# A third of the modulation products moved from VectorE to GpSimd and ScalarE, with weight slots from a free list

## The chip, the cores and the metric

The kernel runs on one core of a Trainium2 chip. The metric is the device time of one launch in microseconds (us); before the change it is 2290.78 us, the median of three runs from 2289.36 to 2290.9. Engines are named as in the profile: PE is TensorE (PEld its weight loads), DVE VectorE, ACT ScalarE, POOL GpSimd, SP the engine whose queue issues the transfers.

## What is computed

A decoder trunk of two layers over 256 tokens with 2048 features, all in float32. Each layer is a token mixer (a gated linear recurrence in layer 0, sparse attention in layer 1) followed by an MLP; so there are four sub-layers, s = 0 to 3. Every sub-layer is modulated by a shift, a scale and a gate that come from one conditioning vector:

```python
cond = jax.nn.silu(c)
mod = jnp.einsum('bd,jde->bje', cond, ada_w[layer]) + ada_b[layer]
shift, scale, gate = jnp.split(mod, 3, axis=-1)
h = x * (1.0 + scale[:, 0, None]) + shift[:, 0, None]
y = mixer(h)
x = _layer_norm(DN_ALPHA * x + (1.0 + gate[:, 0, None]) * y, ln_w, ln_b)
h = x * (1.0 + scale[:, 1, None]) + shift[:, 1, None]
y = sq_relu_mlp(h, mlp_w1, mlp_w2)
x = _layer_norm(DN_ALPHA * x + (1.0 + gate[:, 1, None]) * y, ln_w, ln_b)
```

The modulation needs, per sub-layer, 3 x 2048 dot products of length 2048 with `cond`: a matrix of weights is read once for a single vector.

## The kernel before

**The stream.** Some 620 MB of weights pass through the kernel once. They come as a list of items, most of them a unit of 128 partitions x 2048 numbers (1 MB), in an order written out in `build`: `merge` lays one list evenly into another. `Builder.prefetch` issues a unit's transfer on SP's queue (L104) into one of six slots of the tile `raw`, in turn, while fewer than six are in hand. `Builder.pump` takes the units in the order of the stream:

- A unit of modulation weights (kind "a", input `in_ada`, 192 of them: 48 for each sub-layer, in three parts of 16) holds 128 outputs, one on a partition. One DVE instruction (L120) multiplies it with `cond`, which lies on every partition, and its accumulator sums the products into one column of the tile `mod`.
- A unit of a matrix product (kind "w") is split into two float32r parts, half a unit at a time: ACT rounds it into `whi` (L135), DVE subtracts to get `wlo` (L136). They go into a ring of 16 pieces of 512 columns, from which PE takes them: three matmuls (L193 to L195) for each product.

**The order of instructions** is set when the program is built, by a clock of the builder's own: `step` moves it on by a fixed time for each piece that PE takes (1.31 us), a unit counts as arrived 3.0 us after the one before, and generators (`spawn`) are resumed when their time has come. On the chip each engine then runs its queue strictly in that order and waits on semaphores.

**Where modulation is waited for.** When the last unit of a batch is through, a hook runs: `make_ss` makes the columns `hA` and `hB` on DVE (L427 to L436), with which ACT modulates the activations (L454), which are then split (ACT L496, DVE L497) and multiplied. Sub-layer 0 takes its 32 shift and scale units in five groups (`GROUPS0`: 4, 4, 4, 2 and 2 feature tiles, so 8, 8, 8, 4 and 4 units, each followed by the weights of four products for these features). Sub-layer 1 takes them in four groups of 8 (`GROUPS1`), the first one laid into the recurrence before it. All other units (the gates, sub-layers 2 and 3) are laid into the stream of larger products, long before they are needed.

Between the groups of sub-layer 0 and those of sub-layer 1 stands the recurrence (convolution L801, gates L850, scan L873 and the operations between them, on DVE and ACT), with 24 units laid in.

Of the kernel before, what the change touches and what calls it, by code (L numbers as in the profile page):

```python
# [12 lines left out]
AF = mybir.ActivationFunctionType  # L13
OP = mybir.AluOpType
# [16 lines left out]
RAW = 6  # L31
# [5 lines left out]
GROUPS1 = ((0, 4), (4, 8), (8, 12), (12, 16))  # L37
UNIT_US = 3.0


class Item:
    def __init__(self, kind, src, col=None, then=None, width=2048):
        self.kind, self.src, self.col, self.then, self.width = kind, src, col, then, width
        self.group = 0
        self.done = False
        self.run = None
        self.pieces = {"w": width // 512, "g": 2}.get(kind, 0)


class Builder:  # L50
    def __init__(self, ctx, tc, a, out):
        self.tc, self.nc, self.a, self.out = tc, tc.nc, a, out
        nc = self.nc
        self.const = ctx.enter_context(tc.tile_pool(name="const", bufs=1))
        self.pool = ctx.enter_context(tc.tile_pool(name="work", bufs=1))
        self.psum = ctx.enter_context(tc.tile_pool(name="psum", bufs=1, space=PSUM))
        self.dram = ctx.enter_context(tc.tile_pool(name="dram", bufs=1, space=DRAM))
        self.raw = self.const.tile([128, RAW, 2048], F32, name="raw")
        self.whi = self.const.tile([128, RING, 512], F32R, name="whi")
        self.wlo = self.const.tile([128, RING, 512], F32R, name="wlo")  # L60
        self.now = 0.0
        self.tasks = []
        self.items = []
        self.di = self.pi = 0
        self.cons = self.prod = 0
        self.slot = self.inflight = 0
        self.arrive = []
        self.uid = 0

# [1 line left out]
    def t4(self, shape, dtype=F32):  # L71
# [13 lines left out]

# [1 line left out]
    def set_stream(self, items):  # L87
# [7 lines left out]
    def prefetch(self):  # L95
        while self.di < len(self.items) and self.inflight < RAW:
            it = self.items[self.di]
            if it.kind == "d":
                it.run()
            else:  # L100
                it.raw = self.raw[:, self.slot % RAW, :]
                self.slot += 1
                self.inflight += 1
                self.nc.sync.dma_start(out=it.raw[:, :it.width], in_=it.src)  # L104
            last = self.arrive[-1] if self.arrive else 0.0
            self.arrive.append(max(last, self.now + 1.5) + UNIT_US * it.width / 2048)
            self.di += 1

    def pump(self):
        nc = self.nc  # L110
        while self.pi < len(self.items):
            it = self.items[self.pi]
# [5 lines left out]
            r = it.raw  # L118
            if it.kind == "a":
                nc.vector.scalar_tensor_tensor(r, r, self.one, self.cond, op0=OP.mult, op1=OP.mult, accum_out=it.col)  # L120
            elif it.kind == "raw":
# [19 lines left out]
            self.pi += 1  # L141
            self.inflight -= 1
            self.prefetch()
            if it.then:
                it.then()

# [1 line left out]
    def spawn(self, gen, delay=0.0):  # L148
# [28 lines left out]

# [1 line left out]
    def piece(self, i):  # L179
# [6 lines left out]
    def head(self, kind):  # L186
        """The unit that is next in the stream, as it came."""
        self.until(lambda: self.items[self.pi].kind == kind and not self.items[self.pi].done and self.arrive[self.pi] <= self.now)
        return self.items[self.pi], self.items[self.pi].raw
# [20 lines left out]
    def gemm_ws_outer(self, act, dones, kinds, groups):  # L210
        """Several chunks of columns side by side, a few tiles of the contraction at a time."""
        bs = [[self.bank([128, 2, 256], kind) for _ in range(2)] for kind in kinds]
# [13 lines left out]
    def gemm_as(self, act, done, stagger=None, kind="g"):  # L226
        b = [self.bank([128, 512], kind) for _ in range(2)]
        if not stagger:
# [10 lines left out]
            return  # L239
        # the first token tile runs ahead of the second by as many tiles of weights as the ring holds  # L240
        c0 = self.cons
# [16 lines left out]

# [1 line left out]
    def new_act(self):  # L260
# [17 lines left out]
def build(ctx, tc, a, out):  # L278
# [4 lines left out]

# [1 line left out]
    cond = const.tile([128, 2048], F32, name="cond")  # L285
# [22 lines left out]

    # silu(c), on every partition
    ones = const.tile([1, 128], F32, name="ones")  # L310
# [10 lines left out]

# [1 line left out]
    state = {}  # L323

    def ada_items(s, part, tiles=range(16), then=None):
        its = [Item("a", a["ada"][s, part * 16 + k], col=mods[s][:, part * 16 + k:part * 16 + k + 1]) for k in tiles]
        if then:
            its[-1].then = then
        return its

# [22 lines left out]
    def hook(key):  # L353
        return lambda: hooks[key]()
# [16 lines left out]
    for k0, k1 in GROUPS0:  # L371
        ks = range(k0, k1)
        stream += ada_items(0, 0, ks)
        if k0 % 4 == 0:
            stream.append(x_item(k0 // 4))
        stream += ada_items(0, 1, ks, hook(("h0", k0, k1)))
        stream += [w_part("lru_in", (i,), k0, k1) for i in (4, 0, 5, 1)]
# [4 lines left out]
    def ss_group(k0, k1):  # L382
        ks = range(k0, k1)
        return ada_items(1, 0, ks) + ada_items(1, 1, ks, hook(("h1", k0, k1)))

# [13 lines left out]
    m0 = mlp_items(0)  # L399
    stream += merge(m0[16:], ada_items(1, 2, then=hook(("gate", 1))) + ada_items(2, 0) + ada_items(2, 1, then=hook(("ss", 2))) + ada_items(2, 2, then=hook(("gate", 2))))  # L400
    nsa = []
# [11 lines left out]
    nsa += q_items + [W("nsa_out", n, g) for n in range(4) for g in range(4)]  # L413
    stream += merge(nsa, ada_items(3, 0) + ada_items(3, 1, then=hook(("ss", 3))))
    m1 = mlp_items(1)
    stream += m1[:16] + merge(m1[16:96], ada_items(3, 2, then=hook(("gate", 3)))) + m1[96:]

# [1 line left out]
    def ln_cols(s):  # L419
        return cols[:, C_LNW + 16 * s:C_LNW + 16 * s + 16], cols[:, C_LNB + 16 * s:C_LNB + 16 * s + 16]  # L420

    def make_ss(s, k0=0, k1=16):
        """h = zn * hA + hB, with zn the normalized rows before sub-layer s (its input where s is 0)."""
        m = mods[s]
# [19 lines left out]
    def modulate(s, k0, k1, rows, A):  # L444
        """Up to four feature tiles of the transposed rows become the two parts of the modulated ones."""
        make_ss(s, k0, k1)
# [46 lines left out]

# [1 line left out]
    def split(hi, lo, src):  # L495
        SC.activation(hi, src, AF.Copy)  # L496
        V.tensor_tensor(out=lo, in0=src, in1=hi.bitcast(F32), op=OP.subtract)  # L497

# [1 line left out]
    def residual_source(s):  # L500
# [4 lines left out]
    def ln_task(s, z, t, stats, A, fin=None, rows=None):  # L505
        """Normalizes the rows of token tile t and, with A, makes sub-layer s+1's modulated rows, transposed
        (or with rows, the transposed rows alone; or with fin, the last layer norm's w and b, the output)."""
        mv = B.small([128, 2], "mv")
# [79 lines left out]
    def residual_task(s, z):  # L588
        """The output of sub-layer s, zn w + b, goes to memory until the next layer norm."""
        for n in range(4):  # L590
# [11 lines left out]
    def proj(s, A_in, z, A_out, first=True, last=True, fin=None, rows=None, kinds="gggg"):  # L602
        """z += act @ W over four chunks of columns. The last part of a sub-layer applies the gate, adds the
        residual and normalizes."""
        act = B.act_as(A_in)
# [117 lines left out]

    # ================= layer 0: RG-LRU =================
    # softplus(-lambda) from a range-reduced exponential and the series of log1p
    sp2 = const.tile([128, 16], F32, name="sp2")
# [168 lines left out]

    # ================= MLP of layer 0 =================
    B.until(lambda: znT[3] is not None and znT[3][1] == 3)
# [4 lines left out]

    # ================= layer 1: sparse attention =================
    # relative bias by distance: row h, column 127 + distance
    oh = B.t4([33, 512])
# [4 lines left out]

    # compressed keys and values
    kc = const.tile([128, 4, 15], F32, name="kc")
# [4 lines left out]
    def compress(i):  # L917
        """Sixteen of the 32 positions in a block; the other sixteen come with the next unit."""
        j, h = divmod(i, 2)
# [89 lines left out]

    # branch gates  # L1010
    gbank = B.bank([128, 256], "g")
# [26 lines left out]

    # attention
    O = [None] * NK  # L1040
# [8 lines left out]
    def back(t, start, step, n, copies=None):  # L1049
        """The last axis of t walked backwards from start."""  # L1050
        dims = [list(d) for d in t.ap]
        mid = [0, copies] if copies else dims[1]
        return bass.AP(tensor=t.tensor, offset=t.offset + start, ap=[dims[0], mid, [-step, n]])
# [114 lines left out]

    # ================= MLP of layer 1 =================
    z_in = z  # L1170
# [69 lines left out]
```

## Time and profile before

| | before |
|---|---|
| median of the runs shown | 2290.78 us |
| profiled execution, first to last instruction | 2292.0 us |
| PE busy | 2198.1 us (96%) |
| DVE busy | 1672.3 us (73%) |
| ACT busy | 1057.2 us (46%) |
| POOL busy | 0.2 us |
| moved by the transfers | 623.95 MB, mean 272 GB/s |
| modulation units on DVE | 192, 447.7 us in all |

The profile gives no time for the profiled execution but the span of its instructions, 1.2 us above the median of the runs. The shares are means over stages that differ: a share says which engine is full only where it is read stage by stage. PE's busy time counts matmuls that stand in its pipeline waiting for operands, so the number of matmuls in a stretch says more than the busy time.

### The profile page before, as it was taken

To read this page: it belongs to the slowest core of one execution; us is meant where nothing else is said; L and a number is where in the kernel's file an instruction comes from. 1 tells how busy PE (TensorE), PEld (TensorE's weight loads), DVE (VectorE), ACT (ScalarE), POOL (GpSimd) and SP (SyncE) were. 2 spreads that over 40 slices of the span, in tenths; PEclk is the share of its full clock that TensorE was granted. 3 is DMA by queue.
4 is the path that set the end of the run, shared out by engine and by line. 5 is a ranking of instruction groups with operands and counts; after the bars stand their busy time and mean duration, and the time that the engine had idled before them with its cause. 6 is when DMAs were issued, how large, how long until landed. Compare 5 with 4: busy or idle time off the path is not lost.

```text
span 2292.0 us, 33881 instructions
## 1 busy us (share of the span) xinstructions
PE 2198.1 (96%) x13970; PEld 1966.2 (86%) x13970; DVE 1672.3 (73%) x1987; ACT 1057.2 (46%) x1383; POOL 0.2 (0%) x4
## 2 busy tenths in 40 slices
PE   4799998989999999999999999999999999999997
PEld 3798977978998998998789988788989989988986
DVE  8899999886777767778887688668766444454456
ACT  2356644364453453444443355536544534443541
POOL 0000000000000000000000000000000000000000
PEclk9899999999999999999999999999999999999999
DMA  9987888988878878788689775356788555555561
GB/s 371 411 331 286 338 328 322 373 346 341 306 302 321 298 273 310 294 302 319 234 292 349 293 272 214 132 192 219 281 308 307 190 190 189 191 184 185 208 250 37
DMA packets 98218, 623.95 MB, mean 272 GB/s; under 512 B 10909, under 2 KB 13405, under 8 KB 26896
## 3 DMA queue, kind: packets, MB, share of 16 engines
q1 hardware_dynamic: 98064, 621.80, 72.5%
q8 instruction: 109, 1.79, 0.3%
q14 instruction: 45, 0.37, 0.0%
HBM read 613.30 MB, written 8.45 MB: 271 GB/s over the span
## 4 chain that ended last, share of the span: by engine, by line
PE 84%; DVE 11%; ACT 2%; issue 2%; DMA 1%; DVEq 0%; SPq 0%; ACTq 0%
PE g L195 26%; PE g L194 26%; PE g L193 26%; DVE raw L120 5%; DVE wlo L136 2%; PE m L1124 1%; PE m L1090 1%; ACT whi L135 1%; DMA raw<-in_lru_in 1%; DVE s L801 1%; PE m L929 1%; PE m L1116 0%; PE m L1127 0%; DVE s L497 0%; ACT s L454 0%
## 5 line engine op out<-in xcount | busy, mean ns | idle before, releaser
L136 DVE TENSOR_TENSOR wlo<-raw,whi 128x1024 fp32r<-128x1024 f32 x721 | 872.1, 1222 | 512.4 <-ACT whi L135 510.9
L135 ACT ACTIVATE whi<-raw 128x1024 fp32r<-128x1024 f32 x721 | 754.7, 1057 | 911.7 <-PE g L195 454.2
L193 PE MATMUL g<-s,whi 128*128 128x256 f32 (+1 forms) x2768 | 781.1, 283 | 51.6 <-ACT s L496 50.0
L194 PE MATMUL g<-s,whi 128*128 128x256 f32 (+1 forms) x2768 | 780.4, 282 | 5.1 <-DVE s L497 5.1
L195 PE MATMUL g<-s,wlo 128*128 128x256 f32 (+1 forms) x2768 | 780.6, 283 | 3.2 <-DVE wlo L136 3.2
L193 PEld LDWEIGHTS g<-s,whi 128*128 128x128 f32 (+1 forms) x2768 | 523.1, 189 | 59.1 <-ACT s L496 53.0
L193 PE MATMUL g<-whi,s 128*128 128x512 f32 x1376 | 547.4, 398 | 5.4 <-ACT s L496 5.4
L194 PE MATMUL g<-wlo,s 128*128 128x512 f32 x1376 | 544.9, 396 | 0.0
L195 PE MATMUL g<-whi,s 128*128 128x512 f32 x1376 | 544.6, 396 | 0.3 <-DVE s L497 0.3
L194 PEld LDWEIGHTS g<-s,whi 128*128 128x128 f32 (+1 forms) x2768 | 525.8, 190 | 8.9 <-DVE s L497 6.8
L195 PEld LDWEIGHTS g<-s,wlo 128*128 128x128 f32 (+1 forms) x2768 | 525.1, 190 | 4.8 <-DVE wlo L136 3.8
L120 DVE SCALAR_TENSOR_TENSOR raw<-raw,one,cond 128x2048 f32<-128x2048 f32 x192 | 447.7, 2345 | 19.1 <-DMA raw<-in_ada 18.9
L193 PEld LDWEIGHTS g<-whi,s 128*128 128x128 f32 x1376 | 258.9, 188 | 70.2 <-ACT s L496 7.4
L195 PEld LDWEIGHTS g<-whi,s 128*128 128x128 f32 x1376 | 258.7, 188 | 64.8 <-DVE s L497 2.2
L194 PEld LDWEIGHTS g<-wlo,s 128*128 128x128 f32 x1376 | 258.9, 188 | 62.0 <-issue 0.8
L454 ACT ACTIVATE s<-s,hB,hA 128x256 f32<-128x256 f32 x32 | 16.7, 590 | 120.9 <-DVE hA L430 80.4
L194 PE MATMUL m<-s,whi 128*128 128x256 f32 x256 | 71.1, 278 | 0.0
L195 PE MATMUL m<-s,wlo 128*128 128x256 f32 x256 | 71.1, 278 | 0.0
L193 PE MATMUL m<-s,whi 128*128 128x256 f32 x256 | 70.8, 279 | 0.2 <-ACT whi L135 0.2
L497 DVE TENSOR_TENSOR s<-t,s 128x512 fp32r<-128x512 f32 x78 | 52.8, 685 | 1.5 <-ACT s L496 1.3
L675 ACT ACTIVATE t<-g 128x512 f32<-128x512 f32 x58 | 33.9, 588 | 34.7 <-PE g L195 34.7
L193 PEld LDWEIGHTS m<-s,whi 128*128 128x128 f32 x256 | 47.8, 188 | 0.5 <-ACT whi L135 0.4
(189 smaller groups left out, 1048.6 us busy)
## 6 DMA issues: line engine op xcount, KB each, us to landing
raw<-in_mlp_w SPq DMA_DIRECT2D x256, 1024.0 KB, 5.0
raw<-in_ada SPq DMA_DIRECT2D x192, 1024.0 KB, 6.6
raw<-in_lru_in SPq DMA_DIRECT2D x28, 1024.0 KB, 8.4
raw<-in_nsa_kv SPq DMA_DIRECT2D x24, 1024.0 KB, 5.3
raw<-in_lru_out SPq DMA_DIRECT2D x16, 1024.0 KB, 6.3
raw<-in_nsa_q SPq DMA_DIRECT2D x16, 1024.0 KB, 6.5
raw<-in_nsa_out SPq DMA_DIRECT2D x16, 1024.0 KB, 4.9
t<-in_lnrow SPq DMA_DIRECT2D x24, 256.0 KB, 6.2
```

The lines of the kernel that those rows point to most:

```text
L120: nc.vector.scalar_tensor_tensor(r, r, self.one, self.cond, op0=OP.mult, op1=OP.mult, accum_out=it.col)
L135: nc.scalar.activation(hi, src, AF.Copy)
L136: nc.vector.tensor_tensor(out=lo, in0=src, in1=hi.bitcast(F32), op=OP.subtract)
L193: mm(out, lhi, rhi, start=start, stop=False, skip_group_check=True)
L194: mm(out, lhi, rlo, start=False, stop=False, skip_group_check=True)
L195: mm(out, llo, rhi, start=False, stop=stop, skip_group_check=True)
L497: V.tensor_tensor(out=lo, in0=src, in1=hi.bitcast(F32), op=OP.subtract)
L675: SC.activation(r2, banks[b], AF.Relu)
L801: V.scalar_tensor_tensor(o[:, sh:], p[:, :256 - sh], tap(i, j), o[:, sh:], op0=OP.mult, op1=OP.add)
L929: T.matmul(hv, r[:, 128 * l:128 * l + 128], x[:, :, h:15 + h, l], start=(h == 0 and l == 0), stop=(h == 1 and l == 15))
L1090: T.matmul(ps, qT[:, h, 128 * t:128 * t + 128], kT[g // 2][:, g % 2, :, 0:K], start=True, stop=True)
L1124: T.matmul(po, vt[br][:, kt, 128 * g:128 * g + 128], pT[:, br, kt], start=first, stop=False)
```

## The change

Every third unit of modulation weights (counted over the whole program by `turn`) is taken by a generator, `ada_pool`, unless the one before is still on its way: GpSimd multiplies the unit with `cond` in place, and after 5.5 us on the builder's clock (`POOL_US`) ACT copies the products onto themselves with its accumulator, which sums them into the column of `mod`. Meanwhile `pump` goes on with the next units. Since units are no longer finished in the order of the stream, a slot is handed back by number to a free list, and a hook runs when all units of its batch are through, not behind the last one. In the built program 64 of the 192 units go this way. Lines of the changed kernel: transfers L108, DVE's modulation product L130, `whi` and `wlo` L145 and L146, GpSimd's product L164, ACT's sum L166, `hA` and `hB` L456 to L460, modulation L483, split L525 and L526.

```diff
+POOL_EVERY = 3
+POOL_US = 5.5
...
-        self.slot = self.inflight = 0
+        self.free = list(range(RAW))
+        self.turn = 0
         self.arrive = []
         self.uid = 0
+        self.pooled = False
...
-        while self.di < len(self.items) and self.inflight < RAW:
+        while self.di < len(self.items) and self.free:
             it = self.items[self.di]
             if it.kind == "d":
                 it.run()
             else:
-                it.raw = self.raw[:, self.slot % RAW, :]
-                self.slot += 1
-                self.inflight += 1
+                it.slot = self.free.pop(0)
+                it.raw = self.raw[:, it.slot, :]
                 self.nc.sync.dma_start(out=it.raw[:, :it.width], in_=it.src)
...
             if it.kind == "a":
+                self.turn += 1
+                if self.turn % POOL_EVERY == 0 and not self.pooled:
+                    self.pooled = True
+                    self.pi += 1
+                    self.spawn(self.ada_pool(it))
+                    continue
                 nc.vector.scalar_tensor_tensor(r, r, self.one, self.cond, op0=OP.mult, op1=OP.mult, accum_out=it.col)
...
             self.pi += 1
-            self.inflight -= 1
-            self.prefetch()
-            if it.then:
-                it.then()
+            self.release(it)
+
+    def release(self, it):
+        self.free.append(it.slot)
+        self.prefetch()
+        if it.batch:
+            it.batch[0] -= 1
+            if not it.batch[0] and it.batch[1]:
+                it.batch[1]()
+
+    def ada_pool(self, it):
+
+        self.nc.gpsimd.tensor_tensor(out=it.raw, in0=it.raw, in1=self.cond, op=OP.mult)
+        yield POOL_US
+        self.nc.scalar.activation(it.raw, it.raw, AF.Copy, accum_out=it.col)
+        self.pooled = False
+        self.release(it)
...
-        stream += ada_items(0, 0, ks)
+        shift, scale = ada_items(0, 0, ks), ada_items(0, 1, ks)
+        batch_of(shift + scale, hook(("h0", k0, k1)))
+        stream += shift
         if k0 % 4 == 0:
             stream.append(x_item(k0 // 4))
-        stream += ada_items(0, 1, ks, hook(("h0", k0, k1)))
+        stream += scale
...
-        return ada_items(1, 0, ks) + ada_items(1, 1, ks, hook(("h1", k0, k1)))
+        return batch_of(ada_items(1, 0, ks) + ada_items(1, 1, ks), hook(("h1", k0, k1)))
```

The units of sub-layers 2 and 3 are gathered into batches in the same way. The order of the stream itself stays.

Two places show how the queues change. The first is ACT's queue between the first and the second group of sub-layer 0 (`s_...` are activations, `whi` the rounded weights). Before:

```order
L135 ACTIVATE whi<-raw 128x1024
L454 ACTIVATE s_301<-s_301,hB_95,hA_91 128x256 [waits DMAHW0_49,DVE_49]
L454 ACTIVATE s_301<-s_301,hB_95,hA_91 128x256 x3
L135 ACTIVATE whi<-raw 128x1024 [waits DMAHW5_49,PE_49,Activation_49]
L496 ACTIVATE s_465<-s_301 128x1024 [waits Activation_49]
```

and in the changed kernel:

```order
L145 ACTIVATE whi<-raw 128x1024
L166 ACTIVATE raw,mod_87<-raw 128x2048 [waits Pool_49] x3
L483 ACTIVATE s_303<-s_303,hB_95,hA_91 128x256 [waits DMAHW0_49,DVE_49]
L483 ACTIVATE s_303<-s_303,hB_95,hA_91 128x256 x3
L145 ACTIVATE whi<-raw 128x1024 [waits DMAHW5_49,PE_49]
L525 ACTIVATE s_470<-s_303 128x1024 [waits Activation_49]
```

Three sums of GpSimd's products now stand ahead of the group's modulation, each waiting for GpSimd; everything behind them waits too. The second place is DVE's queue in the same group, up to the first `wlo`. Before:

```order
L120 SCALAR_TENSOR_TENSOR raw,mod_87<-raw,one,cond 128x2048 [waits DMAHW6_49,DVE_49]
L120 SCALAR_TENSOR_TENSOR raw,mod_87<-raw,one,cond 128x2048 [waits DMAHW7_49,DVE_49]
L427 TENSOR_TENSOR mod_87<-mod_87,cols 128x4 [waits DVE_49]
L431 COPY hB_95<-mod_87 128x4 [waits DVE_49]
L120 SCALAR_TENSOR_TENSOR raw,mod_87<-raw,one,cond 128x2048 [waits DMAHW1_49]
L120 SCALAR_TENSOR_TENSOR raw,mod_87<-raw,one,cond 128x2048 [waits DMAHW2_49]
L120 SCALAR_TENSOR_TENSOR raw,mod_87<-raw,one,cond 128x2048 [waits DMAHW3_49]
L120 SCALAR_TENSOR_TENSOR raw,mod_87<-raw,one,cond 128x2048 [waits DMAHW4_49]
L427 TENSOR_TENSOR mod_87<-mod_87,cols 128x4 [waits DVE_49]
L430 TENSOR_SCALAR hA_91<-mod_87 128x4 [waits DVE_49]
L136 TENSOR_TENSOR wlo<-raw,whi 128x1024 [waits DMAHW5_49,PE_49,Activation_49]
```

and in the changed kernel:

```order
L130 SCALAR_TENSOR_TENSOR raw,mod_87<-raw,one,cond 128x2048 [waits DMAHW5_49]
L130 SCALAR_TENSOR_TENSOR raw,mod_87<-raw,one,cond 128x2048 [waits DMAHW6_49,DVE_49]
L456 TENSOR_TENSOR mod_87<-mod_87,cols 128x4 [waits DVE_49,Activation_49]
L460 COPY hB_95<-mod_87 128x4 [waits DVE_49]
L130 SCALAR_TENSOR_TENSOR raw,mod_87<-raw,one,cond 128x2048 [waits DMAHW1_49]
L130 SCALAR_TENSOR_TENSOR raw,mod_87<-raw,one,cond 128x2048 [waits DMAHW2_49]
L130 SCALAR_TENSOR_TENSOR raw,mod_87<-raw,one,cond 128x2048 [waits DMAHW4_49]
L456 TENSOR_TENSOR mod_87<-mod_87,cols 128x4 [waits DVE_49,Activation_49]
L459 TENSOR_SCALAR hA_91<-mod_87 128x4 [waits DVE_49]
L146 TENSOR_TENSOR wlo<-raw,whi 128x1024 [waits DMAHW5_49,PE_49,Activation_49]
```

Of the group's eight products five stay on DVE, and the small additions on `mod` (L456), which waited for DVE alone, now wait for ACT's sums as well.

## Rows read from the trace of the kernel before

**Rows 1.** The page: span, and part 1, each engine's busy time.
```profile
span 2292.0 us, 33881 instructions
PE 2198.1 (96%) x13970; PEld 1966.2 (86%) x13970; DVE 1672.3 (73%) x1987; ACT 1057.2 (46%) x1383; POOL 0.2 (0%) x4
```

**Rows 2.** Busy time of each engine by stage; stretch, its length, then engines with counts.
```profile
core 0: us, PE busy (x) PEld busy (x) DVE busy (x) ACT busy (x) POOL busy (x), PEclk, DMA share, GB/s
0.00:34.90 34.90, 7.19 (x8) 2.49 (x8) 29.52 (x67) 3.28 (x3) 0.20 (x4) 1.00 0.92 367
...
67.30:99.70 32.40, 24.81 (x192) 24.31 (x192) 29.16 (x30) 10.60 (x13) 0.00 (x0) 0.89 1.00 404
...
139.00:300.00 161.00, 153.98 (x1090) 144.61 (x1089) 157.54 (x188) 116.70 (x167) 0.00 (x0) 0.99 0.82 314
...
398.90:431.20 32.30, 32.30 (x276) 32.30 (x276) 29.29 (x34) 8.74 (x11) 0.00 (x0) 1.00 0.91 357
431.20:463.60 32.40, 28.30 (x223) 27.68 (x221) 29.18 (x30) 10.61 (x13) 0.00 (x0) 0.95 0.99 386
...
500.00:1110.00 610.00, 610.00 (x3758) 544.13 (x3757) 447.62 (x426) 274.97 (x306) 0.00 (x0) 1.00 0.81 309
```

**Rows 3.** Timeline of DVE, third group of sub-layer 0: start, duration, instruction.
```profile
67.32 0.17 DVE L430 TENSOR_SCALAR hA<-mod 128x4 f32<-128x4 f32 x1
70.57 1.23 DVE L136 TENSOR_TENSOR wlo<-raw,whi 128x1024 fp32r<-128x1024 f32 x1 [3.09 <-ACT whi L135]
...
72.85 8.03 DVE L136 TENSOR_TENSOR wlo<-raw,whi 128x1024 fp32r<-128x1024 f32 x7
80.80 2.35 DVE L120 SCALAR_TENSOR_TENSOR raw<-raw,one,cond 128x2048 f32<-128x2048 f32 x1
...
97.09 2.35 DVE L120 SCALAR_TENSOR_TENSOR raw<-raw,one,cond 128x2048 f32<-128x2048 f32 x1
99.48 0.16 DVE L427 TENSOR_TENSOR mod<-mod,cols 128x4 f32<-128x4 f32 x1
99.68 0.17 DVE L430 TENSOR_SCALAR hA<-mod 128x4 f32<-128x4 f32 x1
```

**Rows 4.** The page, part 5: DVE's modulation products; count, busy time, mean ns, idle before.
```profile
L120 DVE SCALAR_TENSOR_TENSOR raw<-raw,one,cond 128x2048 f32<-128x2048 f32 x192 | 447.7, 2345 | 19.1 <-DMA raw<-in_ada 18.9
```

**Rows 5.** Groups of DVE instructions, 0 to 300 us: two operands, and one.
```profile
L316 DVE TENSOR_TENSOR s<-s,s 1x1024 f32<-1x1024 f32 x2 | 2.4, 1214 | 0.0
...
L315 DVE TENSOR_SCALAR s<-s 1x1024 f32<-1x1024 f32 x2 | 1.3, 673 | 0.0
```

**Rows 6.** Groups of ACT instructions by shape: copies of 512 and 1024, an accumulator's read.
```profile
L496 ACT ACTIVATE s<-t 128x512 fp32r<-128x512 f32 x78 | 47.6, 624 | 0.1
...
L1100 ACT ACTIVATION_READ_ACCUMULATOR s<-s,am 128x1 f32 x64 | 12.1, 189 | 0.0
...
L496 ACT ACTIVATE s<-s 128x1024 fp32r<-128x1024 f32 x11 | 11.5, 1046 | 11.7 <-DVE s L877 11.7
```

**Rows 7.** The chain that ended last, 140 to 300 us: start, length, what.
```profile
146.44 4.76 DVE s L801 x12
...
159.45 2.27 DVE raw L120 x2
...
203.94 2.27 DVE raw L120 x2
...
215.20 1.73 PE g L840 x8
...
267.19 1.11 DVE raw L120
...
269.49 6.35 DMA raw<-in_lru_out
...
289.24 2.35 DVE raw L120 x2
```

**Rows 8.** Timeline of DVE, the last groups of sub-layer 1.
```profile
431.36 0.16 DVE L434 SCALAR_TENSOR_TENSOR hA<-mod,cols 128x4 f32<-128x4 f32 x1
...
434.89 1.22 DVE L136 TENSOR_TENSOR wlo<-raw,whi 128x1024 fp32r<-128x1024 f32 x1 [3.10 <-ACT whi L135]
...
463.81 0.16 DVE L434 SCALAR_TENSOR_TENSOR hA<-mod,cols 128x4 f32<-128x4 f32 x1
```

**Rows 9.** Stretch of 20 us in which the transfers moved most; columns as in Rows 2.
```profile
20.00:40.00 20.00, 0.80 (x2) 0.50 (x2) 16.61 (x31) 4.85 (x8) 0.00 (x0) 1.00 1.01 425
```

More of the change, by code (lines that the diff above doesn't have):

```diff
@@ L38, with __init__ @@
 UNIT_US = 3.0
+POOL_EVERY = 3
+POOL_US = 5.5
 class Item:
-    def __init__(self, kind, src, col=None, then=None, width=2048):
-        self.kind, self.src, self.col, self.then, self.width = kind, src, col, then, width
+    def __init__(self, kind, src, col=None, width=2048):
+        self.kind, self.src, self.col, self.width = kind, src, col, width
+        self.batch = None
         self.group = 0
@@ L323, in build, with batch_of @@
     state = {}
+    def batch_of(its, then):
+        batch = [len(its), then]
+        for it in its:
+            it.batch = batch
+        return its
     def ada_items(s, part, tiles=range(16), then=None):
         its = [Item("a", a["ada"][s, part * 16 + k], col=mods[s][:, part * 16 + k:part * 16 + k + 1]) for k in tiles]
-        if then:
-            its[-1].then = then
-        return its
+        return batch_of(its, then)
     def ready(key):
@@ L399, in build @@
     m0 = mlp_items(0)
-    stream += merge(m0[16:], ada_items(1, 2, then=hook(("gate", 1))) + ada_items(2, 0) + ada_items(2, 1, then=hook(("ss", 2))) + ada_items(2, 2, then=hook(("gate", 2))))
+    stream += merge(m0[16:], ada_items(1, 2, then=hook(("gate", 1))) + batch_of(ada_items(2, 0) + ada_items(2, 1), hook(("ss", 2))) + ada_items(2, 2, then=hook(("gate", 2))))
     nsa = []
@@ L413, in build @@
     nsa += q_items + [W("nsa_out", n, g) for n in range(4) for g in range(4)]
-    stream += merge(nsa, ada_items(3, 0) + ada_items(3, 1, then=hook(("ss", 3))))
+    stream += merge(nsa, batch_of(ada_items(3, 0) + ada_items(3, 1), hook(("ss", 3))))
     m1 = mlp_items(1)
```

## The prediction

> **What bounds the kernel now.** I read the page's busy times first, then the stages, then the timeline of one group in the stages that are not bound by PE.
>
> Over the whole span PE is busy 96% and DVE 73% [rows 1]. PE's own work does not change here, so all that can be won lies in the 94 us in which PE is idle, and in stretches where it is counted busy but gets few matmuls. The stages say where these are [rows 2]. From 500 to 1110 us PE never stops, at a DVE share of 73%: a product less on DVE is worth nothing there. The stretch 398.9 to 431.2 gives PE's full pace, 276 matmuls in 32.3 us, 0.117 us each. The group from 67.3 to 99.7 has only 192 matmuls, 22.5 us of PE's work, in 32.4 us. There DVE is busy 29.2 us and the transfers have a share of 1.00. So two things are nearly full at once, and the reader should see both before asking what a lighter DVE brings.
>
> The timeline shows how DVE fills that group [rows 3]. From `hA` at 67.32 it waits 3.09 us for ACT, runs eight subtractions and a split until 80.80, then eight modulation products 2.27 us apart (80.80 to 99.48 with two small steps), and reaches the next `hA` at 99.68: 32.36 us, DVE standing still for 3.1 of them. The last groups of sub-layer 1 repeat it: `hA` at 431.36 and 463.81, with the same wait of 3.10 [rows 8]. Between, in the recurrence, DVE is busy 157.5 of 161 us [rows 2]; in the chain of waits from 140 to 300 us modulation products stand seven times (the first at 159.45, the last at 289.24), broken by a PE stretch and by a transfer that lands late [rows 7].
>
> **What goes.** 64 of 192 products leave DVE: at 2.27 us each, 145 us of its 1672 [rows 1, 3, 4]. Only those before 500 us can count: 10 in the groups of sub-layer 0, 8 in the recurrence, 8 in the groups of sub-layer 1.
>
> **What comes on GpSimd.** The trace before has GpSimd at 0.2 us, four constants [rows 1]; neither its product nor what it does to DVE is shown, so both are bounded. The duration: at the least what DVE takes, 2.34 us [rows 4]; at the most the 5.5 us that the builder allows (`POOL_US` in the diff). DVE's own rows say what the reading is worth: with one operand it takes 673 ns for 1024 numbers, with two 1214 [rows 5]. So it can read two numbers at a step and the product with two operands uses both ways. An engine with one way needs two passes for the same unit, 2 x 2.34 = 4.7 us. I take 4.7, between the ends and nearest to a count of operands that rows show.
>
> The price for DVE: nothing at the least (GpSimd reads by a way of its own), the whole GpSimd product at the most (DVE's products and subtractions, all with two operands, stand still while it runs). I take the whole, 4.7 us: the unit's 4096 operands per partition have to be read wherever it is multiplied, DVE's two ways are full while it works, and no row shows a third. If the ways are shared at all, nothing can be won: even at 2.34 us a unit costs what it saved. Net per unit where DVE is the bound: 4.7 - 2.27 = +2.4 us.
>
> [...]
>
> **What comes on ACT.** A copy of 512 takes 624 ns and of 1024 takes 1046, so 2048 take 1.9, with 0.19 for reading the accumulator 2.1 us [rows 6]. That is 134 us more on ACT's 1057, beside other work nearly everywhere (ACT has 117 of 161 us even in the recurrence [rows 2]). It shows where a batch's last unit is the third one: units 24 and 72 end a group, and `hA` then waits for GpSimd and for ACT's sum behind it.
>
> **What moves.** SP issues as many transfers as before. A slot lent to GpSimd is held 4.7 + 2.1 instead of 2.3 us, and transfers behind it in SP's queue wait with it. If DVE's period grows, the transfers have time to spare; if DVE gets lighter, this is late next. Free list and batches add no instruction.
>
> **The sum**, against the profiled execution (2292.0; the median of the runs is 1.2 below, and I add to the median):
> - Groups of sub-layer 0: 10 x 2.4 = 24. One of the gaps of 3.1 us is likely taken by a GpSimd product (unit 9 is the first of its group and can be in hand while DVE waits for ACT): +21.
> - Recurrence: a third of seven products on the chain, 2.3 x 2.4: +6.
> - Groups of sub-layer 1: 8 x 2.4 = 19, less one gap: +16.
> - Two groups that end on ACT's sum: 2 x 2.1 = +4.
> - After 500 us: 38 units. From 500 to 1110 21 x 2.4 = 50 us on DVE's 448 make 82%; the ring of 16 pieces, 12 matmuls each, holds 16 x 12 x 0.117 = 22 us of PE's work, more than one hold of 4.7 and a product: 0. Without that cover each hold would cost its 4.7.
>
> Together +47: **2338 us**. With the price at 2.34 it would be +6 (2297), at 5.5 +64 (2355).
>
> **The rivals.**
> *GpSimd has a way of its own: faster.* Then each unit takes 2.27 us off DVE. For it: ACT's copies run beside DVE's subtractions at full pace in every group. Against it: the transfers are as full as DVE. The first group needs none and wins 2 x 2.27 = 4.5. The groups from 34.9 to 139 run at shares of 0.97 to 1.00; at the best pace seen, 425 against 404 GB/s [rows 2, 9], 104 us become at least 99, and I give 3. The recurrence gives 2.3 x 2.27 = 5; of sub-layer 1's three groups the first gives 6, the others fall from 32.4 towards 29.4 (386 against 425 GB/s), 6. Less the 4 for the sums: -20, **2271**.
> *A jam in ACT's queue: much slower.* If DVE, always ready, keeps GpSimd out until DVE itself waits, GpSimd ends later than the builder's 5.5 us; ACT, in order, stands at the sum, behind it stand the modulation and `whi`, and DVE waits for those. Then product and sum lie in line: 4.7 + 2.1 - 2.27 = 4.5 for each of 10 + 2.3 + 8 units, +92: **2383**. It decides once a product waits longer than two DVE products. Against it: DVE already pauses once in each group.
> *A draw.* The holds fall where DVE waits for transfers (19.1 us of idle before its products [rows 4]) and for ACT, and cost what the products saved: within 0.2% of 2291, about what a measurement can tell from no change here.
>
> **How the numbers follow.** Forecast 0.50, jam 0.12, own way 0.30, draw 0.08: slower 0.62, same 0.08, faster 0.30. The forecast's own range is 2297 to 2355. For eight in ten the range has to take in most of the faster rival: 2268 to 2362, which leaves out the jam and the best of the faster cases.
>
> **What would show it.** Right: GpSimd's products at 4 to 6 us; DVE instructions beside them far over 2.35 and 1.22 us, or idle time between them that nothing explains; the period of a group near 39 us; nothing changed from 500 to 1110. Wrong: DVE's mean durations as before while GpSimd runs, and periods of 30 to 31 us (the faster rival); or ACT idle for long before its sums, released by GpSimd, with DVE waiting for `whi` (the jam). A GpSimd product near 2.3 us would also break the price.

## The result, and the profile after

The changed kernel takes **2371.97 us**, the median of four runs from 2370.38 to 2378.46, beside 2290.84 us for the kernel before: a ratio of 1.0358 with a 95% interval of 1.0343 to 1.0372, so 81 us slower. The forecast was 2338 us and at most 2362: the direction is right, the size was put too low. The profiled execution, 2378.46 us, is the longest of the four, so its trace ends 84.7 us behind the one before where the medians are 81 apart. Of all executions behind the times below one is left out, a slow one of 4949.73 us in the run with three fills.

The page of the changed kernel, span, busy times and the groups that the change touches, answers to [rows 1, 4]:

```profile
span 2376.7 us, 33974 instructions
...
PE 2211.9 (93%) x13970; PEld 1976.6 (83%) x13970; DVE 1745.8 (73%) x1859; ACT 1172.2 (49%) x1511; POOL 337.6 (14%) x68
...
L146 DVE TENSOR_TENSOR wlo<-raw,whi 128x1024 fp32r<-128x1024 f32 x721 | 978.9, 1376 | 476.9 <-ACT whi L145 474.4
...
L164 POOL TENSOR_TENSOR raw<-raw,cond 128x2048 f32<-128x2048 f32 x64 | 337.4, 5273 | 1774.8 <-DMA raw<-in_ada 1660.6 <-DVE raw L130 49.7 <-DVE s L526 39.6
...
L130 DVE SCALAR_TENSOR_TENSOR raw<-raw,one,cond 128x2048 f32<-128x2048 f32 x128 | 352.8, 2765 | 52.9 <-DMA raw<-in_ada 52.9
...
L166 ACT ACTIVATE raw<-raw 128x2048 f32<-128x2048 f32 x64 | 122.6, 1915 | 255.7 <-POOL raw L164 255.7
```

DVE has 64 products less and is busy 73 us *longer*. 64 products at 2.27 us were to take 145 us off it; so some 218 us came back, in instructions that did not change: the mean of the remaining products went from 2345 to 2765 ns, that of the subtractions for `wlo` from 1223 (the mean in the run without GpSimd, below) to 1376.

The stages that stood in [rows 2], by the same clock times:

```profile
core 0: us, PE busy (x) PEld busy (x) DVE busy (x) ACT busy (x) POOL busy (x), PEclk, DMA share, GB/s
...
67.30:99.70 32.40, 19.51 (x146) 19.01 (x145) 29.18 (x20) 14.61 (x17) 10.45 (x2) 0.79 0.93 358
...
139.00:300.00 161.00, 151.33 (x1182) 147.28 (x1181) 147.32 (x161) 108.43 (x150) 35.08 (x6) 0.97 0.75 285
...
500.00:1110.00 610.00, 598.46 (x3867) 542.86 (x3866) 465.13 (x372) 317.85 (x367) 111.16 (x22) 0.99 0.81 307
```

In the 32.4 us from 67.3 DVE is busy as long as before (29.18 against 29.16 us), but runs 20 instructions in place of 30. The transfers fell back from 404 to 358 GB/s, from a share of 1.00 to 0.93: they are not full any more. PE's granted clock is lower too, 0.79 of full in the mean of this stretch in place of 0.89, with 146 matmuls in place of 192, and 0.970 in place of 0.987 over the run; what that costs by itself was not tried apart.

The timeline of DVE says what makes its instructions long. First the third group of sub-layer 0, as in [rows 3], then one convolution step of the recurrence, then the last group of sub-layer 1, as in [rows 8]:

```profile
77.79 0.17 DVE L459 TENSOR_SCALAR hA<-mod 128x4 f32<-128x4 f32 x1
81.05 1.23 DVE L146 TENSOR_TENSOR wlo<-raw,whi 128x1024 fp32r<-128x1024 f32 x1 [3.09 <-ACT whi L145]
...
83.33 12.46 DVE L146 TENSOR_TENSOR wlo<-raw,whi 128x1024 fp32r<-128x1024 f32 x7
...
102.71 4.40 DVE L456 TENSOR_TENSOR mod<-mod,cols 128x4 f32<-128x4 f32 x1
...
109.49 6.58 DVE L130 SCALAR_TENSOR_TENSOR raw<-raw,one,cond 128x2048 f32<-128x2048 f32 x1
...
116.38 0.17 DVE L459 TENSOR_SCALAR hA<-mod 128x4 f32<-128x4 f32 x1
...
173.77 4.77 DVE L830 SCALAR_TENSOR_TENSOR s<-g,cols,s 128x255 f32<-128x255 f32 x12 [5.37 <-ACT s L828]
...
487.39 0.16 DVE L463 SCALAR_TENSOR_TENSOR hA<-mod,cols 128x4 f32<-128x4 f32 x1
...
499.96 6.72 DVE L130 SCALAR_TENSOR_TENSOR raw<-raw,one,cond 128x2048 f32<-128x2048 f32 x1
...
508.88 6.70 DVE L130 SCALAR_TENSOR_TENSOR raw<-raw,one,cond 128x2048 f32<-128x2048 f32 x1
...
524.98 0.15 DVE L463 SCALAR_TENSOR_TENSOR hA<-mod,cols 128x4 f32<-128x4 f32 x1
```

And the timeline of GpSimd in the same stretches:

```profile
87.57 4.86 POOL L164 TENSOR_TENSOR raw<-raw,cond 128x2048 f32<-128x2048 f32 x1 [14.52 <-DMA raw<-in_ada]
100.69 6.40 POOL L164 TENSOR_TENSOR raw<-raw,cond 128x2048 f32<-128x2048 f32 x1 [8.26 <-DMA raw<-in_ada]
108.02 5.90 POOL L164 TENSOR_TENSOR raw<-raw,cond 128x2048 f32<-128x2048 f32 x1 [0.94 <-DMA raw<-in_ada]
...
174.06 4.64 POOL L164 TENSOR_TENSOR raw<-raw,cond 128x2048 f32<-128x2048 f32 x1 [20.44 <-DMA raw<-in_ada]
```

Lay one over the other. GpSimd's product that starts at 100.69 ends at 107.09; DVE's addition of 128x4 numbers, which takes 0.16 us elsewhere, starts at 102.71 and ends at 107.11. The product from 108.02 ends at 113.92; a product of DVE that starts at 109.49 takes 6.58 in place of 2.35 and ends at 116.07, 2.15 us later, about its own work. What DVE starts here beside GpSimd's product stands still until GpSimd is through, for 4.2 to 4.4 us, be it four numbers on a partition or 2048; this document calls that a hold. It is mutual: GpSimd's shortest product takes 4.49 us, and 5.90 or 6.40 where DVE's instruction had to end first. In this group three holds (4.43 in the row of seven subtractions, 4.24, 4.23) cost 12.9 us, three products less save 3 x 2.27 = 6.8, and the group is 38.59 us long instead of 32.36: 6.2 longer, where 6.1 come out.

One step is not held. The convolution at 173.77, twelve instructions of which one operand lies in PSUM (`g`), runs at 4.77 us beside a whole GpSimd product, against 4.76 before [rows 7].

How far the program is behind the kernel before, at the same places of it (the n-th matmul of one trace stands against the n-th of the other; the order differs here and there, but up to each of the four matmuls of the table both traces have run the same ones):

| place | before, us | after, us | behind | gained in the part | forecast for it |
|---|---|---|---|---|---|
| last `hA` of sub-layer 0 | 139.0 | 162.0 | 23.0 | +23.0 | +21 and +2 |
| first hook of sub-layer 1, behind the recurrence | 357.3 | 398.4 | 41.1 | **+18.1** | +6 |
| last hook of sub-layer 1 | 463.8 | 525.0 | 61.2 | +20.1 | +16 and +2 |
| matmul 6543, in the first MLP | 1087.5 | 1148.3 | 60.8 | -0.4 | 0 |
| matmul 7076, behind the layer norm | 1200.5 | 1268.9 | 68.4 | **+7.6** | 0 |
| matmul 9458, at the end of the attention | 1561.4 | 1648.3 | 86.9 | **+18.5** | 0 |
| matmul 13483, in the second MLP | 2177.9 | 2262.4 | 84.5 | -2.4 | 0 |

### The profile page after: what moved, and what is told of

It is laid out like the page before. It is cut to its first block, busy times and chain, and to the rows that moved or that the text cites. A ratio compares the mean times of both kernels' runs of the same rounds, so it can differ in the third digit from the quotient of the medians.

```text
span 2376.7 us, 33974 instructions
## 1 busy us (share of the span) xinstructions
PE 2211.9 (93%) x13970; PEld 1976.6 (83%) x13970; DVE 1745.8 (73%) x1859; ACT 1172.2 (49%) x1511; POOL 337.6 (14%) x68
## 4 chain that ended last, share of the span: by engine, by line
PE 74%; DVE 14%; ACT 5%; issue 3%; DMA 3%; POOL 1%; SPq 0%; DVEq 0%; ACTq 0%; POOLq 0%
PE g L218 23%; PE g L216 23%; PE g L217 23%; DVE raw L130 5%; DVE wlo L146 3%; DMA raw<-in_ada 2%; ACT whi L145 2%; DVE s L526 1%; POOL raw L164 1%; PE m L1119 1%; PE m L1153 1%; PE m L958 1%; ACT s L879 1%; DVE s L902 0%; ACT s L483 0%
## 5 line engine op out<-in xcount | busy, mean ns | idle before, releaser
L146 DVE TENSOR_TENSOR wlo<-raw,whi 128x1024 fp32r<-128x1024 f32 x721 | 978.9, 1376 | 476.9 <-ACT whi L145 474.4
L145 ACT ACTIVATE whi<-raw 128x1024 fp32r<-128x1024 f32 x721 | 748.8, 1056 | 723.6 <-PE g L218 383.8
L164 POOL TENSOR_TENSOR raw<-raw,cond 128x2048 f32<-128x2048 f32 x64 | 337.4, 5273 | 1774.8 <-DMA raw<-in_ada 1660.6
L130 DVE SCALAR_TENSOR_TENSOR raw<-raw,one,cond 128x2048 f32<-128x2048 f32 x128 | 352.8, 2765 | 52.9 <-DMA raw<-in_ada 52.9
L166 ACT ACTIVATE raw<-raw 128x2048 f32<-128x2048 f32 x64 | 122.6, 1915 | 255.7 <-POOL raw L164 255.7
L526 DVE TENSOR_TENSOR s<-t,s 128x512 fp32r<-128x512 f32 x78 | 56.2, 726 | 3.4 <-ACT s L525 3.2
L525 ACT ACTIVATE s<-t 128x512 fp32r<-128x512 f32 x78 | 47.7, 624 | 4.1 <-DVE t L590 4.0
```

What stands on the lines that cost most here:

```text
L145: nc.scalar.activation(hi, src, AF.Copy)
L146: nc.vector.tensor_tensor(out=lo, in0=src, in1=hi.bitcast(F32), op=OP.subtract)
L164: self.nc.gpsimd.tensor_tensor(out=it.raw, in0=it.raw, in1=self.cond, op=OP.mult)
L166: self.nc.scalar.activation(it.raw, it.raw, AF.Copy, accum_out=it.col)
```

## The experiments

The theory after this comparison: GpSimd's product and DVE's instructions exclude each other, and each product puts one hold of some 4.4 us into DVE's queue, which is lost wherever DVE's queue sets the pace. The rivals: ACT, in order, stands at its sums; the free list and the order of slots cost something; GpSimd is simply slow.

### The free list alone

```diff
-POOL_EVERY = 3
+POOL_EVERY = 1000
```

> The free list and the batches stay, but all 192 units are multiplied on DVE. Hold (GpSimd's product and DVE's instructions with two operands exclude each other): the loss needs GpSimd, so 2291 within 5 us. Queue (ACT stands at its sums, slots come back late): the same, 2291 within 5. List (the new order of slots and hooks costs by itself): at least 20 us above 2291.

Measured: 2291.97 us, a ratio of 1.0003 (0.9994 to 1.0013). Free list and batches cost nothing that can be measured.

### ACT's sums without GpSimd

```diff
-        self.nc.gpsimd.tensor_tensor(out=it.raw, in0=it.raw, in1=self.cond, op=OP.mult)
```

> GpSimd's instruction is left out, all else stays: the 64 units leave DVE, their slots are lent for as long, ACT sums them (the raw weights: the multiplication with cond is not computed for a third of the modulation columns). Hold: the whole loss goes and DVE's relief shows, 2255 to 2285. Queue, if ACT's sums or the lent slots cost as such: 2320 to 2370; if ACT only suffers from waiting for GpSimd: as under hold.

Measured: 2288.08 us, 0.9985 (0.9975 to 0.9994). The whole loss is gone, so it is GpSimd's product that makes it. The time lies just above the 2255 to 2285 expected: a third of the products less on DVE is worth only 3 us. The stages of this run say why for the groups of sub-layer 0:

```profile
34.90:67.30 32.40, 26.09 (x194) 25.54 (x194) 23.36 (x25) 17.27 (x21) 0.00 (x0) 0.97 1.01 421
67.30:99.70 32.40, 24.57 (x192) 24.13 (x190) 24.41 (x25) 18.06 (x22) 0.00 (x0) 0.87 1.01 419
```

DVE falls to 24 of 32 us, the transfers are full at a share of 1.01, and DVE's timeline shows what it waits for:

```profile
52.40 2.35 DVE L130 SCALAR_TENSOR_TENSOR raw<-raw,one,cond 128x2048 f32<-128x2048 f32 x1 [2.00 <-DMA raw<-in_ada]
...
59.86 2.35 DVE L130 SCALAR_TENSOR_TENSOR raw<-raw,one,cond 128x2048 f32<-128x2048 f32 x1 [2.61 <-DMA raw<-in_ada]
```

At the hooks of the table above this run is early, 7.35 us at the last `hA` of sub-layer 0 (4.07 of them already at the first `hA`), but only 3.34 at the first hook of sub-layer 1 and 6.37 at its last. So the recurrence, with eight products off DVE and no hold, gives 4.0 us back: it lasts 222.2 us where it lasted 218.3. PE has 1423 matmuls to run in this part against 1328 before, left over from the groups.

```profile
131.68 0.17 DVE L458 TENSOR_SCALAR hA<-mod 128x2 f32<-128x2 f32 x1
...
353.92 0.17 DVE L462 SCALAR_TENSOR_TENSOR hA<-mod,cols 128x4 f32<-128x4 f32 x1
```

### Only the first 26 units, only the other 38

```diff
-                if self.turn % POOL_EVERY == 0 and not self.pooled:
+                if self.turn <= 80 and self.turn % POOL_EVERY == 0 and not self.pooled:
```

> GpSimd takes every third unit among the first 80 only (26 products, all up to the groups of sub-layer 1). By PE's lag in the two traces, 61 us of the loss arise there: 2352 within 6 us if the stages add up. If the later stages make up for a delay: below 2340.

and with `self.turn > 80` in its place:

> GpSimd takes every third unit after the 80th only (38 products). The prediction held these to be covered: 2291. By PE's lag in the two traces they cost 24 us, at the layer norm behind the first MLP and in the attention: 2315 within 6 us.

Measured: 2347.21 us for the first 26 (1.0246, 1.0230 to 1.0261; +56) and 2317.78 us for the rest (1.0116, 1.0099 to 1.0133; +27). They add up to 82 us, and the change loses 81. So what the prediction put at nothing, the units after 500 us, is a third of the loss.

### One operand on GpSimd

GpSimd multiplies the weights by 1.0 and does not read `cond`.

```diff
-        self.nc.gpsimd.tensor_tensor(out=it.raw, in0=it.raw, in1=self.cond, op=OP.mult)
+        self.nc.gpsimd.tensor_scalar(it.raw, it.raw, 1.0, None, op0=OP.mult)
```

> GpSimd multiplies the unit in place by the constant 1, one operand from memory in place of two (the multiplication with cond is not computed for a third of the modulation columns). Hold by any reading of GpSimd: DVE's two-operand instructions still end only with GpSimd's instruction; with its duration D the loss shrinks in proportion, 2288 + 84 x D / 4.5, so 2330 if D is half. Hold only between two instructions with two operands each: 2285 to 2292.

Measured: 2371.28 us, 1.0352 (1.0327 to 1.0377), the time of the change. The timelines of GpSimd and of DVE in the second group:

```profile
57.25 6.04 POOL L164 TENSOR_SCALAR raw<-raw 128x2048 f32<-128x2048 f32 x1 [7.61 <-DMA raw<-in_ada]
```

```profile
57.99 5.71 DVE L130 SCALAR_TENSOR_TENSOR raw<-raw,one,cond 128x2048 f32<-128x2048 f32 x1
```

One operand did not make the instruction shorter: its median is 6.03 us, its minimum 5.36, against 5.10 and 4.49 with two. DVE is held 3.4 us (5.71 less 2.35), and not up to the end of GpSimd's instruction: that ends at 63.29, DVE's at 63.70, and DVE's own work is 2.35. The experiment was made to halve the reading time and did not, so it does not price an operand. It shows that one operand is enough for a hold. Behind sub-layer 1 this run is 50 us late where the change is 61, as a shorter hold lets expect; in the layer norm and the attention it loses 32 where the change loses 26. Why it loses more there stays open.

### GpSimd only writes

```diff
-        self.nc.gpsimd.tensor_tensor(out=it.raw, in0=it.raw, in1=self.cond, op=OP.mult)
+        self.nc.gpsimd.memset(it.raw, 0.0)
```

> GpSimd writes zeros over the unit and reads nothing (a third of the modulation columns is not computed). Hold over reading: DVE's instructions keep their 1.22 and 2.35 us beside it, 2285 to 2292, as without GpSimd. Hold by any GpSimd instruction: the same long DVE instructions as in the change, as long as the writing lasts, above 2300.

Measured: 2288.39 us, 0.9986 (0.9977 to 0.9996). The page's groups:

```profile
L146 DVE TENSOR_TENSOR wlo<-raw,whi 128x1024 fp32r<-128x1024 f32 x721 | 874.9, 1223 | 604.4 <-ACT whi L145 600.0
...
L130 DVE SCALAR_TENSOR_TENSOR raw<-raw,one,cond 128x2048 f32<-128x2048 f32 x128 | 299.5, 2345 | 21.3 <-DMA raw<-in_ada 20.6
...
L164 POOL MEMSET raw<- 128x2048 f32 x64 | 116.2, 1815 | 1903.1 <-DMA raw<-in_ada 1832.1
```

DVE's two-operand instructions are at their old means, 1223 and 2345 ns. In the change they are at 1376 and 2765 in the mean, with the multiplication by 1.0 at 1327 and 2620: it is GpSimd's reading that holds them.

### GpSimd's product in four parts

```diff
-        self.nc.gpsimd.tensor_tensor(out=it.raw, in0=it.raw, in1=self.cond, op=OP.mult)
+        for q in range(4):
+            sl = slice(512 * q, 512 * q + 512)
+            self.nc.gpsimd.tensor_tensor(out=it.raw[:, sl], in0=it.raw[:, sl], in1=self.cond[:, sl], op=OP.mult)
```

> The same product in four GpSimd instructions of 512 columns. Hold: each lasts a quarter and stops DVE for a quarter; DVE gets a turn between them, so no DVE instruction is longer than 4 us, but the sum of the holds is the same: 2360 to 2380. Queue: GpSimd ends later, having to be let in four times, and ACT stands longer at its sums: above 2385.

Measured: 2394.43 us, 1.0449 (1.0431 to 1.0466), slower than with whole products. The page's groups:

```profile
L166 POOL TENSOR_TENSOR raw<-raw,cond 128x512 f32<-128x512 f32 x256 | 484.8, 1924 | 1646.0 <-DMA raw<-in_ada 1361.5
...
L168 ACT ACTIVATE raw<-raw 128x2048 f32<-128x2048 f32 x64 | 122.5, 1915 | 424.1 <-POOL raw L166 424.0
```

Each part now waits for DVE anew (it takes 1.25 us at the least, 1.92 in the mean): 4 x 1.92 = 7.7 us for a unit in place of 5.3, and ACT stands 424 us at its sums instead of 256. This is the time of the queue's expectation, not of the hold's, and the sum of the holds is not the same either: DVE is busy 1654.5 us, 115.8 more than beside the fills above (1538.7), where in the change it is 207.1 more. At the last hook of sub-layer 1 the run is as late as the change (61.9 us against 61.2). What it loses beyond the change it loses in the first MLP and the layer norm behind it: it is 71.3 us late at matmul 6543 and 87.2 at 7076. There GpSimd's parts and the transfers into the slots take turns in the chain that ended last:

```profile
917.21 6.08 DMA raw<-in_ada
...
923.42 7.65 POOL raw L166 x4
...
935.34 6.25 DMA raw<-in_ada
```

So a GpSimd product that takes long enough seems to cost by the slot that it keeps, too; no run tries that apart.

### ACT's sum later

```diff
-POOL_US = 5.5
+POOL_US = 12.0
```

> ACT's sum is placed 12.0 us behind GpSimd's product on the builder's clock in place of 5.5, so that ACT stands less at it (slots are lent longer, and fewer units may find GpSimd free). Hold: 2365 to 2385 for as many products. Queue: most of ACT's 256 us of waiting for GpSimd goes and the time falls to 2310 to 2350.

Measured: 2370.71 us, 1.0352 (1.0336 to 1.0367). Only 55 products go to GpSimd here, and ACT still waits 251.3 us for them. The wait that was to be taken away is still there, so this run says nothing about it. The next two do.

### No sum on ACT

ACT's sum is left out, so nobody waits for GpSimd but the slots.

```diff
-        self.nc.scalar.activation(it.raw, it.raw, AF.Copy, accum_out=it.col)
...
+    for m in mods:
+        V.memset(m, 0.0)
```

> GpSimd's 64 products stay, ACT's sums are left out (a third of the modulation columns stays zero), so that ACT never stands waiting for GpSimd; slots are lent as before. Hold alone makes the loss: 2360 to 2375. ACT's waiting makes it, the hold being covered: 2290 to 2310. Both share: between, and the distance to 2288 (no GpSimd) is the hold's part, the distance to 2372 the waiting's.

Measured: 2375.49 us, 1.0364 (1.0348 to 1.0379). The page:

```profile
PE 2210.3 (93%) x13970; PEld 1976.5 (83%) x13970; DVE 1767.9 (74%) x1863; ACT 1059.6 (45%) x1383; POOL 336.4 (14%) x68
...
L164 POOL TENSOR_TENSOR raw<-raw,cond 128x2048 f32<-128x2048 f32 x64 | 336.2, 5254 | 1773.2 <-DMA raw<-in_ada 1613.3
```

Only the slots wait for the product now and 113 us of ACT's work are gone, yet the loss is whole. The holds make it by themselves.

### The delay without the hold

Three fills in place of the product: GpSimd is busy 5.4 us for a unit and ACT's sum waits for it, but nothing is read.

```diff
-        self.nc.gpsimd.tensor_tensor(out=it.raw, in0=it.raw, in1=self.cond, op=OP.mult)
+        for q in range(3):
+            self.nc.gpsimd.memset(it.raw, 0.0)
```

> In place of the product GpSimd writes zeros over the unit three times, some 5.5 us in which it reads nothing (a third of the modulation columns is not computed); ACT waits for the last writing and sums. This is the change's delay without its hold. Hold: 2285 to 2300. ACT's waiting for a late GpSimd as such: 2340 to 2372.

Measured: 2294.54 us, 1.0015 (1.0005 to 1.0026). With DVE's 1225 and 2347 ns as before, a slow GpSimd and ACT's wait behind it cost 6.5 us against the run with ACT's sums alone (2288.08). That is the other side of the last experiment: so much delay by itself is less than a tenth of the loss. It is not all of the change's delay, as ACT stands 99.7 us at its sums here and 255.7 in the change; that the rest of ACT's wait isn't needed for the loss is what the run without sums shows.

### Only the first MLP, only the attention

```diff
-                if self.turn % POOL_EVERY == 0 and not self.pooled:
+                if 80 < self.turn <= 144 and self.turn % POOL_EVERY == 0 and not self.pooled:
```

> GpSimd takes every third of the units 81 to 144, laid into the first MLP (21 products). The prediction's cover (a ring that holds 22 us of PE's work) holds inside the MLP: 2291 to 2294, or up to 2300 if the last of them reach the layer norm behind it. If the cover fails: each product costs up to 4.4, so up to 2380.

and with `144 < self.turn <= 176`:

> GpSimd takes every third of the units 145 to 176, laid into the sparse attention (11 products). If holds on a chain of waits that runs through DVE cost their whole 4.4 us and a delay is not made up: by the lag in the trace 2308 to 2318. If the ring covers them as predicted: 2291.

Measured: 2292.69 us for the MLP (1.0006, 0.9997 to 1.0015), 2317.81 us for layer norm and attention (1.0104, 1.0086 to 1.0122; +26). In the MLP 22 products make 19 instructions of DVE longer, by 70 us in sum, and nothing is lost: PE's share of the stretch is whole, as it was [rows 2].

```profile
500.00:1110.00 610.00, 610.00 (x3757) 544.11 (x3756) 460.77 (x381) 310.40 (x347) 104.43 (x21) 1.00 0.80 307
```

In layer norm and attention ten products cost 26 us. (The profiled execution, 2311.18 us, is 6 us below the other three, so its trace shows less of it: 7.8 behind the layer norm, 19.7 at the end of the attention.) The chain that ended last, in this run, has

```profile
1348.51 4.19 DVE cm L1095
...
1392.28 4.06 DVE cm L1095
```

and GpSimd's timeline has, at the same places,

```profile
1348.11 4.55 POOL L164 TENSOR_TENSOR raw<-raw,cond 128x2048 f32<-128x2048 f32 x1 [14.63 <-DMA raw<-in_ada]
...
1391.76 4.55 POOL L164 TENSOR_TENSOR raw<-raw,cond 128x2048 f32<-128x2048 f32 x1 [39.10 <-DMA raw<-in_ada]
```

L1095 bounds four numbers on a partition from below in the softmax, 0.17 us of work. Held, it stands on the chain 4.1 us.

## Why the prediction was right and where it failed

**Right: the price of a product.** It took the product at 4.7 us and the hold as whole; the product takes 4.49 us undisturbed, the minimum of the trace, and a hold 4.2 to 4.4. The groups, where DVE sets the pace, came out at +23 and +20 against 23 and 18, with a period of 38.6 us against "near 39". The working behind the 4.7, two passes for two operands, is not borne out: with one operand GpSimd took longer, 5.36 us at the least. The ways, two of DVE and one of GpSimd, were an estimate from the 673 and 1214 ns of [rows 5]; no run shows them. As far as the runs show, that so close a number came of it was luck.

**Right: ACT's sum** at 1.92 and 0.18 us, and the first MLP at 0.

**Failed: "Recurrence: a third of seven products on the chain, 2.3 x 2.4: +6."** It is +18. The term counted only products that stood on the chain before and took off each what it saved there. But GpSimd's product also holds other steps that DVE runs at that moment (the first four below by 4.3 to 4.4 us), and many steps of the recurrence on the chain are DVE's. The chain of the changed kernel there, and further on:

```profile
205.54 6.74 DVE s L902 x4
...
261.57 4.90 DVE s L886
...
285.35 6.64 DVE raw L130 x2
...
341.15 5.48 DVE s L526
...
1211.32 3.90 DVE s L526
...
1304.40 4.54 DVE cu L972
...
1412.36 4.31 DVE cm L1095
...
1456.22 3.77 DVE cm L1095
```

Four of the eight products of this part hold a step on the chain: the scan (2.42 us for its four pieces elsewhere), L886 and L526 (1.2 each), a product (2.35). At 4.4 us that is 17.5, near the +18.1 of the table, without anything taken off for the products that DVE no longer runs there. The run without GpSimd's instruction agrees: with the same products gone and no hold, the part is 4.0 us longer than before, not shorter. So a gross term, holds on the chain times 4.4, comes nearer than a net one. That 17.5 and 18.1 lie so close shows less: PE has 62 matmuls more to run in this part than before (1390 against 1328), and against the run without GpSimd's instruction (222.2 us) the part, 236.4 us, is 14.2 longer; how the rest divides stays open.

**Failed: "After 500 us: 38 units. [...] the ring of 16 pieces [...] holds [...] 22 us of PE's work, more than one hold [...]: 0."** True in the first MLP and in the second for whole products, where DVE feeds PE through the ring and nothing else. Between them lie the layer norm and the attention, where DVE's small steps wait for PE's results and PE for theirs (in the changed kernel L1120 waits 9.9 us for PE in sum, and PE at L1145 4.0 us for DVE); no ring lies between. There the change loses 7.6 and 18.5 us, by the four last rows above among others. The prediction read one stage, 500 to 1110 us, and let it stand for all that followed. It even gave the price without the cover ("each hold would cost its 4.7") but not the places where it applies. In the attention the four rows do not make up the whole 18.5: a transfer and a GpSimd product that ACT waits for, 4.63 us, stand on the chain too, and how the rest divides was not tried apart.

With +18 for the recurrence and +26 for the later stages, the prediction's own sum of 47 becomes 85; 81 were measured.

**The faster rival was priced too high** as well, 2271 us, and so the low end of the range. Without any hold the same relief gives 2288. In the groups of sub-layer 0 that rival had it right: 4.1 us in the first and 3.3 in the others were won, against 4.5 and 3, the transfers being full in those others. It failed in the recurrence, 4.0 us lost in place of 5 won, and in the groups of sub-layer 1, 3.0 us won in place of 12. The jam in ACT's queue, 2383, came nearest in time but is not the cause: without the sum the loss stays whole, and with GpSimd as long at work but no hold it is all but gone.

No version that uses GpSimd in this way beats the kernel before. The two that came out 2 to 3 us below it leave the product out.

## What to carry to other kernels

Book an elementwise operation on GpSimd that reads SBUF as time on DVE, up to GpSimd's own duration (here 4.2 to 4.4 of 4.5 us for a product of two tiles, 3.4 of 6.0 for a multiplication by a constant), and go through every stage in which it may fall: the hold hits what DVE runs then (the convolution's steps, with an operand in PSUM, went free here, 4.77 us against 4.76), and is lost in full wherever that is on the chain, however small the instruction (L1095, 0.17 us of work, stood there 4.1). A buffer between two engines covers a hold only for work that passes through it, and as long as the buffer is filled in time (here -0.4 us in the first MLP, +18.5 in the attention); look for the stages in between, where results go back and forth. And before valuing a lighter engine, read the next resource that is full in the same stretch: here, with the transfers full in the first groups (a share of 1.01) and PE full from 500 to 1110 us (busy in all 610), 3 us were left of a relief of 145.

## What the runs showed of the hardware that was not expected

- **A hold by the product of two tiles did not depend on the length of the held instruction.** 128x4 numbers waited 4.2 us, 128x2048 waited 4.4.
- **A DVE instruction with one operand was held too, and even by a GpSimd that only writes:** up to 4.1 us by a product, 1.1 by the fill below. L1095 (TENSOR_SCALAR, 128x4 in SBUF, a constant as the other operand) is the case in the chain above. In the run where GpSimd only fills, the timelines of GpSimd and of DVE show it again:

```profile
1371.83 1.81 POOL L164 MEMSET raw<- 128x2048 f32 x1 [40.03 <-DMA raw<-in_ada]
...
1372.39 1.26 DVE L1095 TENSOR_SCALAR cm<-cm 128x4 f32<-128x4 f32 x1
```

The fill ends at 1373.64, the step at 1373.65. It happened there to three steps of this kind and to a subtraction behind one of them, 3.9 us in sum, and cost nothing measurable (2288.39 us against 2288.08 without GpSimd's instruction).
- **GpSimd waited for DVE in turn.** Its products took 4.49 us at the least and up to 8.57 (the longest starts at 233.35 and ends 4.5 us behind DVE's last subtraction before it), the parts of a split product 1.25 at the least and up to 6.00.
- **One operand was no cheaper than two on GpSimd:** a multiplication by a constant took 5.36 us at the least, the product of two tiles 4.49; a fill took 1.81.
